# Four equal first chunks, constants on another queue, and two steps moved back in a decoder layer on one core

## Chip, cores, metric

The kernel runs on one core of a Trainium2 chip. The metric is the device time of one execution in microseconds (us). A core has TensorE (matrix products; the profile calls it PE, and PEld its weight loads), VectorE (DVE), ScalarE (ACT), GpSimd (POOL) and SyncE (SP). Here SyncE only issues transfers. ScalarE can issue transfers too, on a queue of its own. Products accumulate in eight banks of 512 float32 columns each.

## What is computed

One layer of a decoder, for 512 tokens of width 1024, all in float32:

```python
x = x + token_mixer(rmsnorm(x, norm_mix_g), w_in, fox_b_f, t5_bias, w_gate, w_branch, w_out)
x = x + conv_ffn(rmsnorm(x, norm_ffn_g), w_up, conv_w, conv_b, w_down)
return rmsnorm(x, norm_final_g)

def rmsnorm(x, g):
    return x * rsqrt(mean(x * x, axis=-1) + 1e-6) * g

def token_mixer(xn, ...):
    proj = xn @ w_in          # queries, keys, values of four mixers, forget gate, indexer
    # stick-breaking, MoBA, forgetting (FoX) and indexer-selected (DSA) attention
    mixed = sum(sigmoid(xn @ w_gate[i]) * (branch[i] @ w_branch[i]) for i in range(4))
    return mixed @ w_out
```

FoX adds to each score the difference of a running sum c of log-sigmoids of its gate logits: + c at the query, - c at the key.

## The kernel before, in words

Each float32 operand is split into a high part (a rounded copy in the format that TensorE takes) and a low part (the rest), and each product is done as three: high by high, low by high, high by low.

**The start.** x arrives transposed, as eight blocks of 128 features by 512 tokens. The first product wants the values of FoX and DSA and the indexer's weights: 328 columns of w_in, also in eight blocks. `CHUNKS` (L880) cuts both into chunks; each chunk of x goes to `xr`, each chunk of weights to `w0r` (L191 to L195). The 28 columns of constants that are wanted first (the norms' gains among them) and the four constant matrices go to `cst` (L190, L196). SP issues nearly all of this, ScalarE two weight chunks. Meanwhile TensorE does nine products of zeros (L199, `WARM`). For every block, ScalarE multiplies x by the gain of the feature, which gives the high part `xhi` (L224), and VectorE makes the low part `xlo` (L227); ScalarE casts the chunk's weights to `w0h` (L226), VectorE makes `w0l` (L229). TensorE then does, chunk by chunk, the three products of each block with four tiles of 128 tokens (L233).

**The mean of squares.** The products take x before its division by the root mean square, and `rstd` is multiplied in later. ScalarE squares x in pairs of blocks (L238), VectorE adds the squares (L242, L244), and a product with a constant matrix (L279) gives the mean over features. `rms_rstd` (L137 to L148) makes rstd of it on ScalarE and VectorE. This product stands behind the first six of the 24 products of the projection `dk` (L276 to L279; DSA key, indexer key and forget gate). The generator of a projection pauses after every six products.

**The projections.** Projections (`proj`, L258) write in turn to two banks (tag "mm"): dk, ix0, ix1, F0q, F0k and so on, so that ix1 takes the bank of dk and F0k that of ix1. After dk, VectorE multiplies rstd in (L266), takes rstd to token rows (L285), and dk's bank is read by copies for `kD` and `ixk` (L363 to L367) and last by the forget gate's first step (L390). `ixtile` (L355) does one of two indexer query projections: rstd on VectorE (L266), high part `iqs` on ScalarE (L358), low part on VectorE (L359), and a transfer to a scratch in DRAM (L360).

**The decay rows.** From the gate row come c's high and low parts `ch` (L399, L400) and their negation `cn` (L401), and both go to DRAM (L402, L403). `fox_fill` (L311) later copies rows of them into the FoX queries and keys.

TensorE's order is that of the program text. The instructions of the other engines are put in order by a scheduler that simulates a timeline, within what data, buffers, `tc.high_priority` and `tc.issue_after` (not before that instruction is issued) allow. Big weights stream through two raw buffers from L100, are cast by ScalarE (L90) and completed by VectorE or GpSimd (L91). After the mixers come the gates, the branch products, the output projection and the feed-forward part.

Of the kernel before, what the change touches and what calls it, by code (L numbers as in the profile page):

```python
# [12 lines left out]
AF = mybir.ActivationFunctionType  # L13
# [3 lines left out]
P = 128  # L17
# [27 lines left out]
def fr(ap):  # L45
    return ap.bitcast(F32)
# [3 lines left out]
def trunk(ctx: ExitStack, tc: tile.TileContext, xt, wv0, wv, wp, wdk, wg, wb, wo, wu, wd,  # L50
          convp, foxb, t5, onehot, consts, ymask, out):
    nc = tc.nc
    V, A, G, T, SP = nc.vector, nc.scalar, nc.gpsimd, nc.tensor, nc.sync
# [7 lines left out]
    cst = cp.tile([P, NCST], F32, name="cst")  # L61
# [44 lines left out]
    def weight(hold=1, ahead=2):  # L106

        i = used[0]
        used[0] += hold
        while len(ready) < min(len(stream), i + hold + ahead):  # L110
            emit_weight()
        return ready[i] if hold == 1 else ready[i:i + hold]

    def dense_steps(o, hi, lo, xh, xl, kt=KT, late=False, chunk=6):


        blocks = [range(kt - 1), [kt - 1]] if late else [range(kt)]
        todo = [(a, b, k) for ks in blocks for a, b in ((hi, xh), (hi, xl), (lo, xh)) for k in ks]
        for n, (a, b, k) in enumerate(todo):
            T.matmul(o, a[:, k], b(k), start=(n == 0), stop=(n == len(todo) - 1))  # L120
            if n % chunk == chunk - 1:
                yield chunk * S / 2400.0

    def blocks_of(t):
        return lambda k: t[:, k]
# [4 lines left out]
    def bank(name, tag="a"):  # L130
        return psum.tile([P, S], F32, name=name, tag=tag, bufs=6 if tag == "a" else 2)
# [46 lines left out]
    with ExitStack() as ph:  # L178
# [8 lines left out]
        w0d = wv0.rearrange("p (k n) -> p k n", k=KT)  # L187
        w0r = []
        with tc.high_priority(offset=5000):
            SP.dma_start(cst[:, 4 * P:], consts[:, 4 * P:NCST])  # L190
            for a, b in CHUNKS:  # L191
                SP.dma_start(xr[:, :, a:b].rearrange("p h k t -> p h (k t)"),
                             xt[:, :, a:b, :].rearrange("h p k t -> p h (k t)"))
                w0r.append(hp.tile([P, b - a, NV0], F32, name=f"w0r{a}", tag="w0r", bufs=4))
                (SP if a > 1 else A).dma_start(w0r[-1], w0d[:, a:b])  # L195
            SP.dma_start(cst[:, :4 * P], consts[:, :4 * P])  # L196
        A.preload_act_table_set("natural_log_exp_and_others")
        wps = bank("wps")
# [22 lines left out]
        sqs, last_hi = [], []  # L221
        for c, (a, b) in enumerate(CHUNKS):
            for k in range(a, b):
# [6 lines left out]
            for m, (x, w) in enumerate(((xhi, w0h), (xlo, w0h), (xhi, w0l))):  # L230
                for k in range(a, b):
                    for tt in range(NB):
                        T.matmul(vps[tt], x[:, k, tt * P:(tt + 1) * P], w[:, k], start=(m == 0 and k == 0),  # L233
                                 stop=(m == 2 and k == KT - 1))
        for c, (a, b) in list(enumerate(CHUNKS))[1:]:
            sq = hp.tile([P, 2, S], F32, name=f"sq{b}", tag="sq", bufs=4)
            with tc.issue_after(last_hi[min(c + 1, len(CHUNKS) - 1)]):
                A.activation(sq.rearrange("p k (h t) -> p h k t", h=2), xr[:, :, b - 2:b], AF.Square)  # L238
            sqs.append(sq)
            if len(sqs) > 1:  # L240
                with tc.issue_after(last_lo):
                    V.tensor_tensor(out=sqs[0], in0=sqs[0], in1=sq, op=OP.add)  # L242
# [15 lines left out]
        def proj(name, m=P):  # L258

            hi, lo = weight()  # L260
            ps = bank(f"d{name}", "mm")
            yield from dense_steps(ps[:m], hi, lo, blocks_of(xhi), blocks_of(xlo))
            return ps[:m]

        def factored(ps):
            V.tensor_tensor(out=ps, in0=ps, in1=rstd[:ps.shape[0]], op=OP.mult)  # L266
            return ps

        def drain(gen):
            while True:  # L270
                try:
                    next(gen)
                except StopIteration as e:
                    return e.value

        dk = proj("dk", 100)  # L276
        next(dk)
        ms = bank("ms")
        T.matmul(ms, onesd, sqa, start=True, stop=True)  # L279
# [75 lines left out]
        def ixtile(c):  # L355
            t = factored(drain(proj(f"ix{c}")))
            hl = pp.tile([P, 2, S], F32R, name=f"iqs{c}", tag="lo", bufs=HB)
            A.copy(hl[:, 0], t)  # L358
            V.tensor_tensor(out=hl[:, 1], in0=t, in1=fr(hl[:, 0]), op=OP.subtract)  # L359
            SP.dma_start(iqd[4 * c:4 * c + 4].rearrange("h b x s -> (h b) x s"), fr(hl))  # L360

        kD = pp.tile([P, 1, 2, S], F32R, name="kD")
        A.copy(kD[0:64, 0, 0], dkp[0:64])  # L363
# [6 lines left out]
        SP.dma_start(fr(kD[64:128, 0]), fr(kD[0:64, 0]))  # L370

        ixtile(0)

        for c0, c1 in ((0, 512), (512, 640)):
# [14 lines left out]
        R4 = slice(96, 100)  # L389
# [7 lines left out]
        ch = pp.tile([P, 2, S], F32R, name="ch", tag="hi", bufs=HB)  # L397
        cn = pp.tile([P, 2, S], F32R, name="cn", tag="lo", bufs=HB)
        A.copy(ch[R4, 0], fw[R4, 0])  # L399
        V.tensor_tensor(out=ch[R4, 1], in0=fw[R4, 0], in1=fr(ch[R4, 0]), op=OP.subtract)  # L400
        A.activation(cn[R4], fr(ch[R4]), AF.Copy, scale=-1.0)  # L401
        SP.dma_start(crd[0], fr(ch[R4]))  # L402
        SP.dma_start(crd[1], fr(cn[R4]))  # L403

        ixtile(1)

        def bias_head(h):
            e = pp.tile([P, S], F32, name=f"e{h}", tag="e", bufs=3)
# [230 lines left out]
        for pr in ("F0", "S0", "F1", "S1", "M0", "M1", "D0", "D1"):  # L639
            nm, b = pr[0], "FMSD".index(pr[0])  # L640
# [207 lines left out]
    for f in range(KT):  # L848
        ch = weight(3, 1)
# [27 lines left out]
PRIO = 60  # L877
RBUFS, WBUFS = 2, 3
HB = 3
CHUNKS = ((0, 1), (1, 2), (2, 4), (4, 6), (6, 8))  # L880
WARM = 9
NV0 = 328
DCH = ((0, 8), (8, 8), (16, 6))
# [13 lines left out]
NCST = 4 * P + 3 * KT + 4  # L897
# [95 lines left out]
```

## Time and profile before

| | us |
|---|---|
| median of three runs | 857.58 (857.57 to 859.62) |
| the profiled execution | 857.41 |
| its span, first to last instruction | 855.6 |
| TensorE busy | 837.3 |
| VectorE busy | 538.1 |
| ScalarE busy | 398.8 |
| GpSimd busy | 164.6 |

The profile is one execution. Its times count from the start of the span. In a timeline's row stand the start, the time that the row's instructions took, the engine, the line of the kernel, the operation, output and inputs by name, shapes and count; in brackets how long the engine had idled before it and what ended that. A group of like instructions stands in one row. Engine "SPq" is SP's issuing of transfers. In a row of windows stand each engine's busy time in that stretch with the number of instructions, then the clock that TensorE was granted (1.00 is 2.4 GHz, 0.50 is 1.2 GHz), the share of the transfer engines' time and the GB/s moved.

### The profile page before, as it was taken

How to read it: one execution, taken by the hardware profiler on the slowest of the kernel's cores; microseconds unless marked ns; L12 is line 12 of the kernel's file. 1: busy time of each engine (PE TensorE's matmuls, PEld its weight loads, DVE VectorE, ACT ScalarE, POOL GpSimd, SP SyncE). 2: the span in 40 equal slices, each digit the busy share in tenths (PEclk: the TensorE clock that was granted, in tenths of full speed). 3: DMA queues.
4: the chain of work that ended last, by engine and by line, in shares of the span. 5: the costliest groups of instructions: out<-in, count | busy, mean ns of one | idle time of the engine just before them, and what ended most of it. 6: DMA issues, size and time to landing. Idle time of an engine off the chain costs nothing.

```text
span 855.6 us, 10625 instructions
## 1 busy us (share of the span) xinstructions
PE 837.3 (98%) x4019; PEld 702.2 (82%) x4019; DVE 538.1 (63%) x931; ACT 398.8 (47%) x612; POOL 164.6 (19%) x131
## 2 busy tenths in 40 slices
PE   8999999999999999999999999999999999999995
PEld 7778887888888888888888888888888888888885
DVE  5947899996453468455554477777777777333234
ACT  6556785664554843232344454444444444232231
POOL 1244575377568300000001200000000000000000
PEclk9999999999999999999999999999999999999998
DMA  6567334326332243232223223333333333333322
GB/s 227 167 163 178 100 132 108 87 58 189 90 120 74 75 130 117 74 103 96 77 74 107 89 98 98 99 99 99 98 99 99 98 97 91 90 93 93 90 65 98
DMA packets 31667, 90.68 MB, mean 106 GB/s; under 512 B 3384, under 2 KB 8376, under 8 KB 31616
## 3 DMA queue, kind: packets, MB, share of 16 engines
q1 hardware_dynamic: 30240, 88.62, 34.3%
q10 hardware_dynamic: 1376, 1.38, 0.5%
q8 instruction: 31, 0.51, 0.2%
q14 instruction: 20, 0.16, 0.1%
HBM read 83.78 MB, written 5.82 MB: 105 GB/s over the span
## 4 chain that ended last, share of the span: by engine, by line
PE 80%; DVE 1%; POOL 0%; ACT 0%; issue 0%; DVEq 0%; POOLq 0%
PE u L120 28%; PE dg L120 19%; PE dn L833 14%; PE o L120 5%; PE b L120 5%; PE vpsVM L303 1%; PE dM1q L120 1%; PE dM1k L120 1%; PE zb L545 1%; PE dD1q L120 1%; PE dD0q L120 1%; PE ptD L484 1%; PE ptM L484 1%; PE dM0q L120 0%; PE oD L500 0%; PE oM L500 0%
## 5 line engine op out<-in xcount | busy, mean ns | idle before, releaser
L90 ACT CAST wh<-wr 128x1024 fp32r<-128x1024 f32 (+1 forms) x129 | 133.7, 1039 | 153.8 <-PE dn L833 70.4
L91 DVE TENSOR_TENSOR wl<-wr,wh 128x1024 fp32r<-128x1024 f32 (+2 forms) x97 | 116.3, 1200 | 138.6 <-ACT wh L90 63.6
L120 PE MATMUL u<-xhi,wh 128*128 128x512 f32 x352 | 87.5, 390 | 0.0
L91 POOL TENSOR_TENSOR wl<-wr,wh 128x1024 fp32r<-128x1024 f32 x32 | 77.0, 2408 | 52.9 <-PE dix L120 15.3
L120 PE MATMUL u<-xlo,wh 128*128 128x512 f32 x352 | 87.1, 389 | 0.0
L120 PE MATMUL u<-xhi,wl 128*128 128x512 f32 x352 | 87.1, 389 | 0.0
L809 DVE SCALAR_TENSOR_TENSOR cv<-h,cvp,cv 128x511 f32<-128x511 f32 x88 | 66.0, 751 | 26.2 <-ACT cv L807 24.6
L120 PEld LDWEIGHTS u<-xhi,wh 128*128 128x128 f32 x352 | 66.1, 188 | 14.1 <-issue 0.5
L120 PEld LDWEIGHTS u<-xlo,wh 128*128 128x128 f32 x352 | 66.1, 188 | 13.7
L120 PEld LDWEIGHTS u<-xhi,wl 128*128 128x128 f32 x352 | 66.1, 188 | 13.7
L807 ACT ACTIVATE cv<-h,cvp 128x512 f32<-128x512 f32 x44 | 35.9, 815 | 79.8 <-DVE h L805 79.8
L833 PE MATMUL dn<-mh,wh 128*128 128x512 f32 (+1 forms) x198 | 72.9, 368 | 0.0
L833 PE MATMUL dn<-ml,wh 128*128 128x512 f32 (+1 forms) x198 | 72.3, 365 | 0.0
L833 PE MATMUL dn<-mh,wl 128*128 128x512 f32 (+1 forms) x198 | 72.3, 365 | 0.0
L120 PE MATMUL dg<-xlo,wh 128*128 128x512 f32 x256 | 66.1, 392 | 0.0
L120 PE MATMUL dg<-xhi,wh 128*128 128x512 f32 x256 | 64.9, 390 | 0.0
L120 PE MATMUL dg<-xhi,wl 128*128 128x512 f32 x256 | 64.3, 390 | 0.0
L120 PEld LDWEIGHTS dg<-xhi,wl 128*128 128x128 f32 x256 | 47.7, 188 | 9.8
L120 PEld LDWEIGHTS dg<-xhi,wh 128*128 128x128 f32 x256 | 47.8, 188 | 9.4
L120 PEld LDWEIGHTS dg<-xlo,wh 128*128 128x128 f32 x256 | 47.4, 188 | 9.5
L781 POOL TENSOR_TENSOR rstd<-rstd,sqo 128x512 f32<-128x512 f32 x7 | 9.1, 1302 | 187.1 <-ACT sqo L780 187.1
L833 PEld LDWEIGHTS dn<-ml,wh 128*128 128x128 f32 x198 | 37.3, 188 | 6.2
(430 smaller groups left out, 1453.0 us busy)
## 6 DMA issues: line engine op xcount, KB each, us to landing
wr<-in_wu SPq DMA_DIRECT2D x44, 512.0 KB
wr<-in_wg SPq DMA_DIRECT2D x32, 512.0 KB
wr<-in_wp SPq DMA_DIRECT2D x16, 512.0 KB
wr<-in_wd SPq DMA_DIRECT2D x16, 512.0 KB
wbr<-in_wb SPq DMA_DIRECT2D x8, 512.0 KB
wr<-in_wo SPq DMA_DIRECT2D x8, 512.0 KB
wr<-in_wd SPq DMA_DIRECT2D x8, 384.0 KB
bdram<-brd SPq DMA_DIRECT2D x2, 1280.0 KB
```

Source lines behind the costliest of these rows:

```text
L90: A.copy(hi, raw)
L91: eng.tensor_tensor(out=lo, in0=raw, in1=fr(hi), op=OP.subtract)
L120: T.matmul(o, a[:, k], b(k), start=(n == 0), stop=(n == len(todo) - 1))
L303: T.matmul(ps, a[:, k, ts_], b, start=(m == 0), stop=(m == 3 * KT - 1))
L484: T.transpose(pt[:, (i - j) * P:(i - j + 1) * P], z[:, QOFF[i] + P * j:QOFF[i] + P * (j + 1)], ident)
L545: T.matmul(zs[j][:, P * (j2 - j):n], trir if j2 == j else negr, x[:, KOFF[j2]:KOFF[j2] + n2], start=False, stop=(j2 == NB - 1 and x is ll) ...
L781: G.tensor_tensor(out=acc, in0=acc, in1=sq, op=OP.add)
L807: A.activation(c, h, AF.Identity, scale=cvp[:, i, 2:3], bias=cvp[:, i, 3:4])
L809: V.scalar_tensor_tensor(out=c[:, x:], in0=h[:, :S - x], scalar=cvp[:, i, 2 - x:3 - x], in1=c[:, x:], op0=OP.mult, op1=OP.add)
L833: T.matmul(o, a, b[:, k, cs], start=(n == 0 and m == 0), stop=(n == ND - 1 and m == 2))
```

## The change

x and the first weights come in four chunks of two blocks instead of two of one block and three of two. SP's first transfer is x. ScalarE issues the first weight chunk and then the 28 columns of constants; SP issues the other weight chunks. The squares still come in four pairs of blocks. A second `next(dk)` puts twelve of dk's products ahead of the mean of squares. `ixtile` returns the instruction that makes the high part, and the negation `cn` is issued only after that of ix1; ix1's projection now stands ahead of the negation and its transfer in the text.

```diff
@@ -187,12 +187,13 @@
         with tc.high_priority(offset=5000):
-            SP.dma_start(cst[:, 4 * P:], consts[:, 4 * P:NCST])
             for a, b in CHUNKS:
                 SP.dma_start(xr[:, :, a:b].rearrange("p h k t -> p h (k t)"),
                              xt[:, :, a:b, :].rearrange("h p k t -> p h (k t)"))
                 w0r.append(hp.tile([P, b - a, NV0], F32, name=f"w0r{a}", tag="w0r", bufs=4))
-                (SP if a > 1 else A).dma_start(w0r[-1], w0d[:, a:b])
+                (SP if a else A).dma_start(w0r[-1], w0d[:, a:b])
+                if a == 0:
+                    A.dma_start(cst[:, 4 * P:], consts[:, 4 * P:NCST])
             SP.dma_start(cst[:, :4 * P], consts[:, :4 * P])
@@ -232,7 +233,7 @@
-        for c, (a, b) in list(enumerate(CHUNKS))[1:]:
+        for c, (a, b) in enumerate(CHUNKS):
@@ -274,6 +275,7 @@
         dk = proj("dk", 100)
+        next(dk)
         next(dk)
         ms = bank("ms")
@@ -355,9 +357,10 @@
-            A.copy(hl[:, 0], t)
+            hi = A.copy(hl[:, 0], t)
             V.tensor_tensor(out=hl[:, 1], in0=t, in1=fr(hl[:, 0]), op=OP.subtract)
             SP.dma_start(iqd[4 * c:4 * c + 4].rearrange("h b x s -> (h b) x s"), fr(hl))
+            return hi.ins
@@ -398,11 +401,11 @@
-        A.activation(cn[R4], fr(ch[R4]), AF.Copy, scale=-1.0)
         SP.dma_start(crd[0], fr(ch[R4]))
+
+        with tc.issue_after(ixtile(1)):
+            A.activation(cn[R4], fr(ch[R4]), AF.Copy, scale=-1.0)
         SP.dma_start(crd[1], fr(cn[R4]))
-
-        ixtile(1)
@@ -877,7 +880,7 @@
-CHUNKS = ((0, 1), (1, 2), (2, 4), (4, 6), (6, 8))
+CHUNKS = ((0, 2), (2, 4), (4, 6), (6, 8))
```

## Rows read from the trace of the kernel before

**Rows 1.** The page's table of busy time: TensorE.

```profile
PE 837.3 (98%) x4019; PEld 702.2 (82%) x4019; DVE 538.1 (63%) x931; ACT 398.8 (47%) x612; POOL 164.6 (19%) x131
```

**Rows 2.** Who waited for whom, TensorE, whole span: total, times, longest.

```profile
PE vpsVM L303 <- DVE vvM L211: 1.3, 1, 1.3
```

**Rows 3.** Timeline of all engines, 0 to 40 us: TensorE's first products.

```profile
1.32 4.16 PE L200 MATMUL wps<-warm 128*128 128x512 f32 x9 [1.32 <-POOL warm L186]
...
6.75 0.87 PE L233 MATMUL vps<-w0h,xhi 128*128 128x328 f32 x4 [1.28 <-ACT xhi L224]
...
11.42 1.47 PE L233 MATMUL vps<-w0h,xhi 128*128 128x328 f32 x8 [0.65 <-ACT w0h L226]
```

**Rows 4.** TensorE's timeline, 21 to 30 and 34 to 49 us.

```profile
22.34 1.54 PE L120 MATMUL ddk<-xhi,wh 128*100 128x512 f32 x6
24.59 1.12 PE L279 MATMUL ms<-sqa,cst 128*128 128x512 f32 x2 [0.71 <-DVE sqa L244]
...
36.43 2.11 PE L120 MATMUL dix<-xhi,wh 128*128 128x512 f32 x8
...
48.08 1.21 PE L120 MATMUL dF0k<-xhi,wh 128*128 128x512 f32 x4 [0.48 <-DVE iqs L359]
```

**Rows 5.** Timeline of all engines, 0 to 40 us: SP's issues and ScalarE.

```profile
0.74 0.40 SPq L190 DMA_DIRECT2D cst<-in_consts  x1
...
1.20 1.45 SPq L192 DMA_DIRECT2D xr<-in_xt  x3
...
5.98 0.72 ACT L224 ACTIVATE xhi<-xr,cst 128x512 fp32r<-128x512 f32 x1 [2.28 <-DMA xr<-in_xt]
...
7.51 0.73 ACT L224 ACTIVATE xhi<-xr,cst 128x512 fp32r<-128x512 f32 x1 [0.46 <-DMA xr<-in_xt]
...
12.23 1.32 ACT L224 ACTIVATE xhi<-xr,cst 128x512 fp32r<-128x512 f32 x2
...
15.05 1.32 ACT L224 ACTIVATE xhi<-xr,cst 128x512 fp32r<-128x512 f32 x2
```

**Rows 6.** Windows at the start: last column GB/s.

```profile
0.00:2.00 2.00, 0.68 (x2) 0.59 (x3) 0.25 (x3) 0.33 (x1) 1.36 (x7) 1.00 0.07 9
0.00:5.60 5.60, 4.16 (x9) 2.81 (x9) 0.75 (x4) 1.75 (x2) 2.81 (x9) 1.00 0.63 157
0.00:7.50 7.50, 4.90 (x13) 3.40 (x13) 1.52 (x6) 2.83 (x4) 2.81 (x9) 1.00 0.70 181
8.00:11.00 3.00, 2.78 (x19) 2.51 (x17) 1.59 (x3) 1.84 (x4) 0.00 (x0) 1.00 1.05 408
```

**Rows 7.** Timelines of VectorE and ScalarE, 26 to 49 us.

```profile
27.54 0.69 DVE L144 SCALAR_TENSOR_TENSOR tm<-ms,rstd 128x512 f32<-128x512 f32 x1
...
35.28 0.76 DVE L390 TENSOR_SCALAR fw<-ddk,fb 4x512 f32<-4x512 f32 x1
...
43.62 1.98 DVE L400 TENSOR_TENSOR ch<-fw,ch 4x512 fp32r<-4x512 f32 x1
47.33 0.69 DVE L359 TENSOR_TENSOR iqs<-dix,iqs 128x512 fp32r<-128x512 f32 x1 [1.73 <-ACT iqs L358]
...
45.63 1.06 ACT L401 ACTIVATE cn<-ch 4x1024 fp32r<-4x1024 f32 x1 [2.13 <-DVE ch L400]
46.72 0.59 ACT L358 CAST iqs<-dix 128x512 fp32r<-128x512 f32 x1
```

**Rows 8.** Window from the first FoX keys to 200 us.

```profile
48.00:200.00 152.00, 147.61 (x833) 127.35 (x834) 127.05 (x319) 102.96 (x190) 83.77 (x55) 1.00 0.44 121
```

**Rows 9.** Windows at the end of the span: granted clock before the last two columns.

```profile
842.00:845.00 3.00, 3.00 (x28) 3.00 (x27) 2.77 (x5) 0.00 (x0) 0.00 (x0) 1.00 0.35 115
845.00:848.00 3.00, 1.08 (x6) 0.47 (x4) 0.78 (x2) 1.30 (x3) 0.00 (x0) 1.00 0.70 235
848.00:849.00 1.00, 0.00 (x0) 0.00 (x0) 0.90 (x3) 0.00 (x1) 0.00 (x0) 0.68 0.00 0
849.00:855.00 6.00, 0.00 (x0) 0.00 (x0) 2.87 (x5) 0.00 (x0) 0.00 (x0) 0.50 0.53 175
```

## The prediction

> **What bounds the kernel now.** I read the page's table of busy time first. TensorE works for nearly the whole span [rows 1], so the change can win only what TensorE now idles or spends out of turn. The list of TensorE's waits is second: twelve causes, none over 1.3 us [rows 2], some 9 us in all. Four lie before 48 us, where the change acts, and TensorE's own timeline dates them. The first product of the real weights starts at 6.75 after 1.28 us of idling, the third chunk (blocks 2 and 3) at 11.42 after 0.65 [rows 3], the mean of squares at 24.59 after 0.71, and the projection of the first FoX keys at 48.08 after 0.48 [rows 4]. Then come ScalarE's timeline, which shows when each chunk of x was in hand [rows 5], the bytes moved by then [rows 6], and VectorE's and ScalarE's timelines between 27 and 48 us, which show what the later starts depend on [rows 7].
>
> The profiled execution took 857.41 us, span 855.6 and 1.8 around it, 0.17 under the median of the three runs, 857.58. I make the sum in microseconds won or lost in the profile and apply it to the median. What a measurement of this kernel can tell from no change is about 0.3%, 2.57 us.
>
> **Step 1, the first transfers.** The constants leave the head of SP's queue, so x is issued at 0.74 instead of 1.20 [rows 5]; on ScalarE's queue they take the place of the second weight chunk, so ScalarE issues two transfers as before. Chunk 0 is now 512 KB of x and 328 KB of weights; with 14 KB of constants that is 874 kB. The first product needs all of x's chunk where it needed half.
>
> When is that in hand? By 5.60 us the queues had moved 5.60 x 157 = 879 kB [rows 6]: were every byte for chunk 0, it would be there at about 5.6, the early bound. The late bound is the old kernel itself: the second block of x, the last of the same bytes, released ScalarE at 7.51 [rows 5]. I take the middle, 6.55: the first end has no straggler, in the second later chunks have mixed in, and the new case is neither. The Trainium skill (DMA: Bandwidth & Descriptors, section Anatomy of one DMA) gives a transfer a fixed part of about 2 us and the rest at 436 GB/s: an estimate from that page has 874 kB there 4 us after the issue, near 5.1, and the sum would be 855.4, close to the second rival below. The rows gave 157 to 181 GB/s on average up to there [rows 6].
>
> The constants follow 328 KB of weights on ScalarE's queue, and every scaling of x reads a gain from them. I cost this at nothing, because x's 512 KB should end later than the 342 KB there. If that cover fails, the loss is bounded by the same 7.51: by then the old kernel had all these bytes.
>
> **Step 2, the chunk stage.** TensorE followed ScalarE's first scaling by 0.77 us (5.98 to 6.75) [rows 3, 5], so its first product starts at 7.32 (6.37 to 8.28). From the third chunk on, nine groups of eight products took 11.42 to 22.34, 1.213 us each [rows 3, 4]. Twelve such groups are 14.56 and end at 21.9 (20.9 to 22.85), against 22.34. Removed are the 0.65 us wait and small gaps, added is the later start. Call the shift s: **-0.45 us**, between -1.4 and +0.5. ScalarE went round a middle chunk in 2.82 us (12.23 to 15.05) [rows 5] against TensorE's 3.64, so it keeps up.
>
> **Step 3, the mean of squares.** It now stands behind twelve products of the first projection instead of six. A product of 512 columns takes 0.233 us (48 of them from 36.43 to 47.60) [rows 4]. The mean of squares started 2.25 us after that projection (22.34 to 24.59); six products are 1.40, so 0.85 was lost there, and the later place removes it. But twelve products take 2.80, so it starts 0.55 us later, plus s. All of rstd's chain on VectorE hangs on it, from 27.54 to the end of the forget-gate row at 35.28 + 0.76 = 36.04 [rows 7], and VectorE's instructions follow close on one another in between. That row is the last reader of the bank into which the second indexer projection (ix1) writes: the small banks alternate between two, and dk and ix1 share one. TensorE would reach ix1 at 36.43 - 0.85 + s = 35.13, while the bank comes free at 36.04 + 0.55 + s = 36.14. It waits a microsecond there, and with 0.06 for the release (47.33 + 0.69 to 48.08 [rows 4, 7]) starts at 36.20. So steps 2 and 3 together are worth 36.43 - 36.20 = **0.23 us**; the 0.85 has turned into a wait ten microseconds later. At the ends of s the pair gives a gain of 1.18 or a loss of 0.72.
>
> **Step 4, the negated rows.** Now ScalarE does the negation (45.63, 1.06 us) ahead of ix1's high part (46.72), though its input is ready only when VectorE ends the decay's low part at 43.62 + 1.98 = 45.60 [rows 7]. ix1's high part waits behind it, its low part follows at 47.33, and the bank that this frees lets the first FoX keys go at 48.08, 0.48 late [rows 4, 7]. With the high part first, ScalarE does it in the idle 2.1 us before 45.63, and the low part can end near 46.3. TensorE arrives near 47.4, so the whole **0.48 us** goes. Behind the negation stand its transfer, on SP the copies of the decay rows and the next weights, on ScalarE a weight cast. It still starts when its input ends, so I cost these at nothing; were it to follow the high part late, by its 0.59 us [rows 7], the cover is that the rows are not read before the first scores, after the whole projection of the FoX keys.
>
> **Step 5, after 48 us.** VectorE is busy 127.05 of 152 us up to 200 [rows 8], and TensorE waits on chains that start from its own results. I let the gain pass whole.
>
> Sum: -0.23 - 0.48 = -0.71, or **856.9 us**. Its own range runs from 857.58 - 1.18 - 0.48 = 855.9 to 857.58 + 0.72 - 0.48 = 857.8.
>
> **The rivals.**
>
> *The array's clock falls before the first product: slower.* The idling between the warm-up (done at 1.32 + 4.16 = 5.48) and the first product grows from 1.28 to 1.84 us, at most 2.8 [rows 3]. At the end of this trace TensorE was full to 845, worked 1.08 us of the next three, and the granted clock then fell from 1.00 to 0.50, the 1.2 GHz level, within the microsecond from 848 [rows 9]. So a gap of 1.28 us did not do it, three microseconds with little work did, and the new gap lies between. The warm-up ran at 4.16 / 9 = 0.46 us a product, twice 0.233, for 4.16 us. If the first real products ran at that level as long, half of it, 2.08 us, would be lost: 856.9 + 2.08 = **859.0**. The Trainium skill (TensorE: Matmul & The Clock Gate, section HAM oscillation — how this bites in real kernels) says that an array kept waiting by transfers between bursts is throttled again and starts the next burst cold; by that rule this rival would be the forecast. The old gap did not show it, the end of the trace did. Chance 0.20; it decides if the first product comes at the late end of step 2.
>
> *The first transfers run at the later rate.* If the short rows of the two small chunks made the start slow, 874 kB at the 408 GB/s of 8 to 11 us take 2.1 us; next to nothing has moved by 2.0 [rows 6], so they are there near 4.1. Then s is -2.9, and the sum 857.58 - 2.9 + 0.22 - 0.48 = **854.4**. Against it, 7.50 x 181 = 1357 kB had moved by 7.50 [rows 6], some 480 of them from the third chunk with its long rows, and the average was still so low. Chance 0.07.
>
> *VectorE has more room than I think.* All engines but TensorE are put in order by the program's scheduler, and an order with the forget-gate row earlier would spare the wait of step 3. Then -0.45 - 0.85 - 0.48 = -1.78, **855.8**; with the early bound of step 1, 854.85. VectorE's packed row speaks against it [rows 7]. Chance 0.08.
>
> *Nothing arrives at the end.* The gain is eaten between 48 and 200 us, where VectorE is nearly full [rows 8] and a wait such as the 1.3 us for the MoBA values [rows 2] grows by as much, or a late landing costs in steps 2 and 3 what step 4 wins: **857.6**. Chance 0.15.
>
> **How the numbers follow.** The forecast has 0.50. Faster than 855.0 needs the rate rival (0.05 of its 0.07), VectorE's room with an early landing (0.02) or an order of the other engines that I can't see (0.03): 0.10. Slower than 860.15 needs the low clock for longer together with a late landing (0.04), or a worse order (0.03): 0.07. Within 0.3%: 0.83. The range leaves out the faster cases below and the low clock with a late landing above, about 0.10 on either side: 855.0 to 859.3.
>
> **What would show it.** Right: ScalarE's first scaling near 6.6 and released by x, TensorE's twelve groups in 14.6 us without a stop, no wait at the mean of squares, a new wait of about 1 us ahead of ix1, none ahead of the FoX keys, and those near 47.4. Wrong: a first scaling at 7.5 or released by the constants, early groups of 2.4 us, no wait ahead of ix1, another order on VectorE before 40 us, or TensorE's waits after 48 us grown by what was won.

## The result and the profile after

The changed kernel takes 862.61 us (median of 6 runs, 860.55 to 865.13), the one before 857.58 (6 runs, 857.38 to 859.62). The ratio is 1.0057 [1.0034, 1.008], slower, and the median lies above the range given. Ratios and intervals here are those of the comparison itself, not quotients of medians. The profiled execution took 861.86 us, span 860.1, against 855.6 before: 4.5 us to be found in one trace.

The page's table of busy time, the row that answers to [rows 1]:

```profile
PE 840.1 (98%) x4019; PEld 705.5 (82%) x4019; DVE 537.2 (62%) x930; ACT 398.5 (46%) x611; POOL 164.3 (19%) x131
```

TensorE does the same 4019 products, but is busy 2.8 us longer: part of the loss is products that ran more slowly. The rest is waiting, and the list of who waited for whom (total, times, longest) has a new first row; the 1.3 us of [rows 2] stand unchanged below it:

```profile
PE dix L120 <- DVE fw L393: 3.5, 1, 3.5
```

The timeline of the changed kernel dates it. First ScalarE and TensorE at the start (answering to [rows 3, 5]), then TensorE from dk to the first FoX keys (answering to [rows 4]):

```profile
1.21 0.45 ACTq L196 DMA_DIRECT2D cst<-in_consts  x1
1.32 4.21 PE L201 MATMUL wps<-warm 128*128 128x512 f32 x9 [1.32 <-POOL warm L186]
5.92 1.34 ACT L225 ACTIVATE xhi<-xr,cst 128x512 fp32r<-128x512 f32 x2 [0.41 <-DMA cst<-in_consts]
6.70 2.56 PE L234 MATMUL vps<-w0h,xhi 128*128 128x328 f32 x8 [1.17 <-ACT xhi L225]
9.05 1.79 PE L234 MATMUL vps<-w0h,xlo 128*128 128x328 f32 x8
...
22.68 2.00 PE L120 MATMUL ddk<-xhi,wh 128*100 128x512 f32 x8
25.45 1.02 PE L281 MATMUL ms<-sqa,cst 128*128 128x512 f32 x2
34.62 1.24 PE L379 MATMUL bp<-vt,t5s 32*8 32x512 f32 x4
39.37 3.75 PE L120 MATMUL dix<-xhi,wh 128*128 128x512 f32 x8 [3.51 <-DVE fw L393]
47.13 1.98 PE L120 MATMUL dF0q<-xhi,wh 128*128 128x512 f32 x8
52.57 0.61 PE L120 MATMUL dF0k<-xhi,wh 128*128 128x512 f32 x2
```

The kernel before began its FoX queries, which follow ix1, here:

```profile
42.00 1.98 PE L120 MATMUL dF0q<-xhi,wh 128*128 128x512 f32 x8
```

Read as a ledger against [rows 4], in us lost:

| stretch | before | after | lost |
|---|---|---|---|
| up to dk | 22.34 | 22.68 | +0.34 |
| dk until TensorE is free for ix1 | 14.09 (to 36.43) | 13.18 (to 39.37 - 3.51 = 35.86) | -0.91 |
| wait ahead of ix1 | 0 | 3.51 | +3.51 |
| ix1's 24 products | 42.00 - 36.43 = 5.57 | 47.13 - 39.37 = 7.76 | +2.19 |
| FoX queries, then the keys | 48.08 - 42.00 = 6.08 | 52.57 - 47.13 = 5.44 | -0.64 |
| sum, at the first FoX keys | 48.08 | 52.57 | +4.49 |

The moves themselves did what they were for: no wait stands at the mean of squares or at the FoX keys. The loss is one place, ix1. Why does its bank come free so late? VectorE's timeline of the changed kernel:

```profile
34.79 1.22 DVE L91 TENSOR_TENSOR wl<-wr,wh 128x1024 fp32r<-128x1024 f32 x1 [0.42 <-ACT vvF L211]
35.93 0.69 DVE L267 TENSOR_TENSOR dix<-dix,rstd 128x512 f32<-128x512 f32 x1
36.53 0.48 DVE L212 SCALAR_TENSOR_TENSOR vvF<-vps,rst,vvF 128x256 fp32r<-128x256 f32 x1
37.04 0.69 DVE L370 TENSOR_TENSOR ixk<-ddk,ixk 32x512 fp32r<-32x512 f32 x1
37.76 0.68 DVE L380 TENSOR_TENSOR vt<-vt,bp 8x512 f32<-8x512 f32 x1
38.47 0.76 DVE L393 TENSOR_SCALAR fw<-ddk,fb 4x512 f32<-4x512 f32 x1
```

and of the kernel before, right behind its forget-gate row at 35.28 [rows 7]:

```profile
36.07 1.22 DVE L91 TENSOR_TENSOR wl<-wr,wh 128x1024 fp32r<-128x1024 f32 x1
37.32 0.70 DVE L266 TENSOR_TENSOR dix<-dix,rstd 128x512 f32<-128x512 f32 x1
...
38.97 0.86 DVE L377 TENSOR_TENSOR vt<-vt,bp 8x512 f32<-8x512 f32 x2
```

Three instructions that stood behind the bank's last reader, fw, now stand ahead of it: the weights' low part 1.22, ix0's rstd 0.69 and the bias row 0.68, together 2.59 us. The first of them comes after 0.42 us of idling, for a vvF of ScalarE. (Of VectorE's own four vvF, three stand ahead of fw in either kernel.) No line of the diff touches these three. The program's scheduler, which orders all engines but TensorE, chose anew once TensorE's order had changed.

The windows of the changed kernel say why ix1 then ran slowly (busy time of PE, PEld, DVE, ACT, POOL, then PEclk, the granted clock, DMA share and GB/s). The last one answers to [rows 8]:

```profile
35.00:37.00 2.00, 0.86 (x4) 0.17 (x2) 2.00 (x3) 1.40 (x5) 0.00 (x0) 1.00 0.53 113
37.00:38.00 1.00, 0.00 (x0) 0.00 (x0) 0.94 (x3) 0.46 (x2) 0.00 (x0) 0.64 0.69 131
38.00:39.30 1.30, 0.00 (x0) 0.00 (x0) 1.24 (x3) 0.04 (x1) 0.00 (x0) 0.50 0.84 328
39.30:44.00 4.70, 4.63 (x11) 3.69 (x12) 4.43 (x13) 2.41 (x5) 0.00 (x0) 0.50 0.33 123
44.00:45.00 1.00, 1.00 (x5) 0.81 (x5) 0.52 (x1) 0.45 (x1) 0.00 (x0) 0.94 0.00 0
...
48.00:200.00 152.00, 147.63 (x833) 127.31 (x832) 123.67 (x306) 101.94 (x184) 84.10 (x54) 1.00 0.42 117
```

Within the pause the granted clock fell from 1.00 to 0.50, the 1.2 GHz level, and it stayed there while ix1 worked without a gap, until just after 44. After 48 us the product count and the busy time of the old kernel are back.

### The profile page after: what moved, and what is told of

The parts are those of the page before. It is cut to its first block, busy times and chain, and to the rows that moved or that the text cites. A ratio compares the mean times of both kernels' runs of the same rounds, so it can differ in the third digit from the quotient of the medians.

```text
span 860.1 us, 10620 instructions
## 1 busy us (share of the span) xinstructions
PE 840.1 (98%) x4019; PEld 705.5 (82%) x4019; DVE 537.2 (62%) x930; ACT 398.5 (46%) x611; POOL 164.3 (19%) x131
## 4 chain that ended last, share of the span: by engine, by line
PE 80%; DVE 1%; POOL 0%; ACT 0%; issue 0%; DVEq 0%; POOLq 0%
PE u L120 28%; PE dg L120 19%; PE dn L836 14%; PE o L120 5%; PE b L120 5%; PE vpsVM L305 1%; PE dM1q L120 1%; PE dM1k L120 1%; PE zb L548 1%; PE dD1q L120 1%; PE dD0q L120 1%; PE ptD L487 1%; PE ptM L487 1%; PE dM0q L120 0%; PE oD L503 0%; PE oM L503 0%
## 5 line engine op out<-in xcount | busy, mean ns | idle before, releaser
L836 PEld LDWEIGHTS dn<-mh,wh 128*128 128x128 f32 x198 | 37.3, 188 | 6.2
```

What stands on the lines that cost most here:

```text
L836: T.matmul(o, a, b[:, k, cs], start=(n == 0 and m == 0), stop=(n == ND - 1 and m == 2))
```

## The experiments

The theory from this trace: the second `next(dk)` alone costs over 4 us, by VectorE's new order and the clock that falls in the pause. The rivals: the chunks cost something too, by late constants or by a low clock at the start; the negation costs or wins something else than its 0.48. The kernel before had medians of 857.63, 857.45 and 857.60 in the three groups of runs (experiments 1 to 4; 5 to 8; 9 to 12), and 857.58 beside the change. Where medians of different groups are compared below, up to 0.2 us of the difference can be the group's.

**1. The mean of squares alone** (against the kernel before):

```diff
         next(dk)
+        next(dk)
```

> Only the second step of dk ahead of the mean of squares, all else as before. Theory (the later mean of squares makes the scheduler put the forget gate's first step behind other work on VectorE, the bank of ix1 comes free some 3.5 us late, and TensorE's clock falls in that pause): 861 to 864.5 us, a wait of 3 to 4 us ahead of ix1, released by the forget gate's step, and a stretch of 1.2 GHz that starts in or just behind it. Rival (the larger first chunks cost the time): 856.5 to 858.5 us and a wait of at most 1.2 us there.

Measured: 861.95 (860.31 to 862.22, 5 runs), ratio 1.0037 [1.0023, 1.005]. Its timeline has the same wait of the same length:

```profile
39.48 3.75 PE L120 MATMUL dix<-xhi,wh 128*128 128x512 f32 x8 [3.51 <-DVE fw L391]
```

One line makes the wait, without the chunks and without the negation. From the start of dk to the FoX keys this trace takes 30.02 us (22.79 to 52.81) where the kernel before took 25.74, 4.28 more; by the medians the line costs 4.32, by the ratio 3.2. VectorE's new order, with the three instructions ahead of fw, was found in the change and in experiments 1, 6 and 9. The kernels without the second `next(dk)` lack it, and so do experiments 5 and 11, which have that line but free the bank.

The start of this trace shows one thing more. Its chunks are the old ones and its first product came after a pause of 1.02 us, and yet the first four products took 1.26 us (6.55 to 7.81), where the kernel before took 0.79: a low clock at the start does not need the larger chunks.

**2. The negation alone** (against the kernel before):

```diff
-        A.activation(cn[R4], fr(ch[R4]), AF.Copy, scale=-1.0)
...
-        ixtile(1)
+        with tc.issue_after(ixtile(1)):
+            A.activation(cn[R4], fr(ch[R4]), AF.Copy, scale=-1.0)
```

> Only the negation behind ix1's high part. Theory: 857.58 - 0.48 = 857.1 us, the wait of 0.48 us ahead of the first FoX keys gone and nothing else moved. Rival (the gain is eaten between 48 and 200 us): 857.6 us with the wait gone and other waits of TensorE grown by as much.

Measured: 857.07 (856.52 to 858.78, 11 runs), ratio 0.9995 [0.9986, 1.0004]. The time alone can't be told from no change; its timeline can:

```profile
47.46 1.98 PE L120 MATMUL dF0k<-xhi,wh 128*128 128x512 f32 x8
...
86.36 3.50 PE L120 MATMUL dF1q<-xhi,wh 128*128 128x512 f32 x8
```

The wait of 0.48 [rows 4] is gone, and ix1 had started at 36.45, as before. But this execution was the slowest of the eleven, 858.78, with a span of 857.0: it lost again more than it had won. TensorE waited 0.4 us for the indexer queries to come back from DRAM (iq from iqd), a wait that the list of the kernel before does not have, and at about 86.5 the granted clock fell:

```profile
87.00:90.00 3.00, 3.00 (x8) 2.31 (x8) 2.48 (x6) 0.90 (x3) 2.79 (x6) 0.52 0.82 266
```

The eight products from 86.36 took 3.29 us to the next group, in the kernel before 1.86. Three of the eleven runs lie near 858.7, the others at 857.22 or less; whether the other two slow ones had the same fall was not traced.

**3. The chunks alone** (against the kernel before; constants and chunks as in the change):

```diff
-            SP.dma_start(cst[:, 4 * P:], consts[:, 4 * P:NCST])
...
+                if a == 0:
+                    A.dma_start(cst[:, 4 * P:], consts[:, 4 * P:NCST])
...
-CHUNKS = ((0, 1), (1, 2), (2, 4), (4, 6), (6, 8))
+CHUNKS = ((0, 2), (2, 4), (4, 6), (6, 8))
```

> Only the four equal chunks, with the constants on ScalarE's queue. Theory (the mean of squares costs the time): 856.5 to 858.5 us, VectorE's order as before, no wait over 1 us ahead of ix1. Rival (the chunks cost it, by a first product that finds TensorE at 1.2 GHz): 859.5 to 862 us, with the loss in the products before 23 us.

Measured: 860.04 (858.8 to 861.45, 11 runs), ratio 1.0023 [1.0014, 1.0033]. My expectation fell, the rival's held. Timeline of ScalarE, then of TensorE:

```profile
5.88 0.74 ACT L227 CAST w0h<-w0r 128x656 fp32r<-128x656 f32 x1 [2.84 <-DMA w0r<-in_wv]
7.75 2.56 ACT L225 ACTIVATE xhi<-xr,cst 128x512 fp32r<-128x512 f32 x4 [1.13 <-DMA cst<-in_consts]
...
8.52 2.56 PE L234 MATMUL vps<-w0h,xhi 128*128 128x328 f32 x8 [2.99 <-ACT xhi L225]
...
25.48 1.55 PE L120 MATMUL ddk<-xhi,wh 128*100 128x512 f32 x6
```

The 14 KB of constants, issued at 1.23, released ScalarE only at 7.75, 1.87 us behind the weights ahead of them on the same queue. TensorE paused 2.99 us and then ran the first group of eight in 2.35 us (8.52 to 10.87), where a full clock takes 1.21 [rows 3, 4]. So dk began 3.1 us late. The change's own trace had hardly shown this: in that execution the constants released ScalarE at 5.92.

What moved meanwhile, from 5.42 to 7.30 (queue; packets, MB, share of the transfer engines' time; q1 is SP's, q10 ScalarE's):

```profile
q1 hardware_dynamic: 232, 0.47, 84.8%
q10 hardware_dynamic: 128, 0.01, 5.8%
```

The weights were through by then, and the packets of the constants went out a few at a time beside SP's transfers. The landings recorded in the same trace, told apart by the order of issue and by when their readers were released, have the first chunk of x complete at 6.18 and the constants at 7.66: x was not what was missing.

**4. Chunks and negation, the change without the second `next(dk)`:**

```diff
-        next(dk)
```

> The change without the second step of dk ahead of the mean of squares: four equal chunks and the negation behind ix1's high part. Theory: 856 to 858 us, 4 to 6 us under the whole change; the sum of what chunks alone and negation alone give. Rival (the chunks cost the time): 859 to 861.5 us.

Measured: 859.07 (858.1 to 859.74, 11 runs), ratio 1.0013 [1.0004, 1.0022]; again the rival's figure.

```profile
7.88 1.34 ACT L225 ACTIVATE xhi<-xr,cst 128x512 fp32r<-128x512 f32 x2 [1.51 <-DMA cst<-in_consts]
...
48.83 1.98 PE L120 MATMUL dF0k<-xhi,wh 128*128 128x512 f32 x8
```

Late constants again, and no wait at the FoX keys. By medians the parts alone cost 4.32 (mean), 2.41 (chunks) and -0.56 (negation), 6.17 in all; the change costs 5.03. So they add up to within 1.1 us, while the change's own runs spread over 4.6.

**5. The whole change, dk's bank freed early.** dk times rstd goes to a tile of SBUF instead of back into the bank, so the bank's last reader is that product and not the forget-gate row (against the change):

```diff
-        dkp = factored(dkp)
+        dks = pp.tile([P, S], F32, name="dks", tag="ir", bufs=3)
+        V.tensor_tensor(out=dks[:100], in0=dkp, in1=rstd[:100], op=OP.mult)
+        dkp = dks
```

> The whole change, but VectorE writes dk times rstd to SBUF, so that dk's bank is free after one instruction and the forget gate's step is no longer what ix1 waits for. Theory (the bank's last reader is the wait of 3.5 us and through it the fall of the clock): the wait ahead of ix1 gone, no stretch of 1.2 GHz between 30 and 50 us, 856.5 to 859.5 us. Rival (the later rstd holds up whatever comes next, bank or not): a wait of 2 us or more at another projection before 60 us and 860.5 us or more.

Measured: 859.12 (856.25 to 860.05, 12 runs), ratio 1.001 [1.0, 1.0021], 3.5 us under the change. Timeline and windows of this kernel:

```profile
8.04 1.33 ACT L225 ACTIVATE xhi<-xr,cst 128x512 fp32r<-128x512 f32 x2 [1.93 <-DMA cst<-in_consts]
...
8.82 2.55 PE L234 MATMUL vps<-w0h,xhi 128*128 128x328 f32 x8 [3.60 <-ACT xhi L225]
...
39.20 2.11 PE L120 MATMUL dix<-xhi,wh 128*128 128x512 f32 x8
```

```profile
8.00:15.00 7.00, 6.18 (x23) 6.18 (x24) 5.66 (x8) 6.96 (x11) 0.00 (x0) 0.51 1.05 405
...
38.00:44.00 6.00, 6.00 (x26) 4.25 (x26) 5.94 (x15) 5.36 (x12) 0.00 (x0) 1.00 0.57 154
```

With the bank free, ix1 follows the bias products without a wait and at the full clock: the wait and the low clock at 37 to 44 have one cause. The edit changes VectorE's order too (fw now comes at 35.55, ahead of ix0's rstd, the weights' low part and the bias row), so it does not part the bank from the order. That the bank is the link is read from the release in the change's trace, `<-DVE fw`, and from the program, in which dk's bank is all that fw and ix1 share. What is left is the start: the nine warm-up products took 3.90 us instead of 4.21, so the last of them had run at the higher clock; then TensorE stood still for 3.60 us, and from 8 to 15 it ran at half. Its times spread over 3.8 us.

**6. The pause filled with products** (20 of 384 columns into the second bias product's bank, behind that product; nothing reads them):

```diff
+        for i in range(20):
+            T.matmul(bp[:, 128:512], xhi[:, i % KT, :P], xhi[:, i % KT, 128:512], start=True, stop=True)
```

> The whole change, with 20 products of 384 columns (some 3.3 us at full clock) into unused columns of a bank ahead of ix1; their results are read by nothing. Theory (3.5 us of the loss is the wait, 2.2 us the clock that falls in it): ix1 starts as late as with the change, 39.4 or so, but at full clock, and the time is 1.8 to 2.8 us under the change's, 859.5 to 861 us. Rival (the clock's fall has another cause, or costs nothing that is not lost anyway): 862 to 864 us.

Measured: 866.48 (863.81 to 867.73, 5 runs), ratio 1.0096 [1.0081, 1.0112], outside both ranges:

```profile
38.55 5.33 PE L382 MATMUL bp<-xhi 128*128 128x384 f32 x20 [3.73 <-DVE vt L380]
```

VectorE reads that bank too (the bias row at line 380), so the filler waited as long as ix1 had and only came behind the pause. The 20 products themselves took 5.16 us to the next group (38.55 to 43.71), in experiment 9, without a pause ahead of them, 3.68 (34.48 to 38.16): behind this pause too some 1.5 us went to the clock, only not in ix1.

**7. Equal chunks, constants back at the head of SP's queue** (against the kernel before, whose first transfer stays where it was):

```diff
-                (SP if a > 1 else A).dma_start(w0r[-1], w0d[:, a:b])
+                (SP if a else A).dma_start(w0r[-1], w0d[:, a:b])
...
+CHUNKS = ((0, 2), (2, 4), (4, 6), (6, 8))
```

> Only the four equal chunks, with the constants at the head of SP's queue as before. Theory (behind the first weights on ScalarE's queue the constants land last, and every scaling of x waits for them): first scaling released by x at 6 to 6.6 us instead of by the constants at 7.8, and 857.5 to 859.3 us, 1 us or more under chunks alone (860.0). Rival (x's larger first chunk is the late one): first scaling at 7.5 us or later, released by x, and 859.5 us or more.

Measured: 857.04 (856.31 to 857.3, 11 runs), ratio 0.9994 [0.9986, 1.0003]: 3.0 us under the chunks alone (2.8 if each is taken against the kernel before of its own group), and a little better than I had expected.

```profile
5.89 1.33 ACT L224 ACTIVATE xhi<-xr,cst 128x512 fp32r<-128x512 f32 x2 [1.07 <-DMA xr<-in_xt]
...
6.66 2.55 PE L233 MATMUL vps<-w0h,xhi 128*128 128x328 f32 x8 [1.14 <-ACT xhi L224]
```

Now x itself releases the first scaling, and the runs spread over 1.0 us instead of 2.7. The queue of the constants, not the size of the chunks, was the cost.

**8. The chunks alone with a longer warm-up** (against experiment 3):

```diff
-WARM = 9
+WARM = 16
```

> Chunks alone with 16 products of zeros ahead instead of 9, so that TensorE works until some 7 us. Theory (of what chunks cost, over 1 us is the clock at 1.2 GHz behind the longer pause): the first products run at full clock, groups of 1.2 us, and 857.6 to 858.9 us, with the first product still near 8.5. Rival (only the later start counts): 859.5 to 861 us. A third way: zeros do not hold the clock, and nothing changes.

Measured: 857.42 (856.09 to 858.0, 11 runs), ratio 0.9995 [0.9986, 1.0003], 2.6 us under the chunks alone.

```profile
1.32 6.69 PE L201 MATMUL wps<-warm 128*128 128x512 f32 x16 [1.32 <-POOL warm L186]
7.84 1.37 PE L234 MATMUL vps<-w0h,xhi 128*128 128x328 f32 x8
9.06 1.36 PE L234 MATMUL vps<-w0h,xlo 128*128 128x328 f32 x8
```

The first product starts later than in the change's trace (7.84 against 6.70), and still dk begins earlier, at 22.24 against 22.68, because the groups take 1.21 us from the first one on. From the first product to dk it is 14.40 us, in experiment 3 16.96. In this execution, 1.0 us under the kernel's median, the constants landed early (they released ScalarE at 6.22), so it shows the clock and not a late landing that was covered. Experiments 7 and 8 each take back about all that the chunks cost, so the late constants and the low clock are not two costs to be added: the late landing makes the pause, and the pause costs most where the clock is low behind it.

**9. The pause filled ahead of the second bias product** (the same 20 unread products):

```diff
+            for i in range(20 if c0 else 0):
+                T.matmul(bp[:, 128:512], xhi[:, i % KT, :P], xhi[:, i % KT, 128:512], start=True, stop=True)
```

> The whole change, with the same 20 unread products put ahead of the second bias product, so that they don't wait for VectorE's reading of their bank. Theory (2.2 us of the loss is the clock that falls in the wait ahead of ix1): ix1 starts near 39.4 as with the change, no stretch at 1.2 GHz after 30 us, and 859.3 to 861.5 us. Rival (the clock's fall there costs nothing that is not lost anyway): 862 to 864 us.

Measured: 860.38 (858.69 to 861.82, 5 runs), ratio 1.0033 [1.002, 1.0046], 2.2 us under the change.

```profile
34.48 3.74 PE L380 MATMUL bp<-xhi 128*128 128x384 f32 x20
...
38.47 2.12 PE L120 MATMUL dix<-xhi,wh 128*128 128x512 f32 x8
...
44.06 1.98 PE L120 MATMUL dF0q<-xhi,wh 128*128 128x512 f32 x8
```

The useless products end about when the bank comes free (fw ends at 38.14), so ix1 starts no earlier after dk than in the change (16.88 us against 16.69), but its 24 products now take 5.59 us (38.47 to 44.06) instead of 7.76. This prices the fall of the clock apart from the wait: 2.17 us in the trace. The 2.2 between the medians agree, but there the intervals overlap and the starts differ as well (dk began at 21.59 here, at 22.68 in the change's trace).

**10. What the runs recommended so far**: equal chunks, constants on SP, the negation moved, 13 warm-up products, the mean of squares where it was (against the change):

```diff
+            SP.dma_start(cst[:, 4 * P:], consts[:, 4 * P:NCST])
...
-                if a == 0:
-                    A.dma_start(cst[:, 4 * P:], consts[:, 4 * P:NCST])
...
-        next(dk)
...
-WARM = 9
+WARM = 13
```

> The parts that should pay: four equal chunks with the constants at the head of SP's queue, the negation behind ix1's high part, 13 products of zeros instead of 9, the mean of squares where it was. Theory: 857.04 (chunks with the constants on SP) less 0.48 for the wait ahead of the first FoX keys, less 0.5 to 1.5 for the first groups at full clock: 855 to 856.1 us. Rival (gains of this size are eaten before the end): 856.7 to 857.5 us.

Measured: 856.1 (855.36 to 857.22, 11 runs), ratio 0.9985 [0.9976, 0.9994], at the upper end of what I had expected.

```profile
23.54 1.13 PE L279 MATMUL ms<-sqa,cst 128*128 128x512 f32 x2 [0.71 <-DVE sqa L244]
...
46.39 1.98 PE L120 MATMUL dF0k<-xhi,wh 128*128 128x512 f32 x8
```

**11. The same with the mean of squares moved and dk's bank freed** (experiment 10 with the second `next(dk)` and the three lines of experiment 5):

```diff
+        next(dk)
...
-        dkp = factored(dkp)
+        dks = pp.tile([P, S], F32, name="dks", tag="ir", bufs=3)
+        V.tensor_tensor(out=dks[:100], in0=dkp, in1=rstd[:100], op=OP.mult)
+        dkp = dks
```

> The same with the mean of squares behind twelve products and dk's bank freed after one instruction. Theory (with equal chunks TensorE no longer waits for the squares, so the later place has nothing to win, and with the bank free nothing to lose): within 0.5 us of the kernel without it. Rival (the later place still wins its 0.85 us): 0.6 us or more faster than that kernel.

Measured: **854.93** (854.54 to 855.26, 7 runs), ratio 0.997 [0.9959, 0.9981], the best kernel here, and 1.17 us under experiment 10. No run of it is as slow as the fastest of experiment 10. I had expected the two to be within half a microsecond; the rival was right.

```profile
24.26 1.02 PE L280 MATMUL ms<-sqa,cst 128*128 128x512 f32 x2
34.60 2.11 PE L120 MATMUL dix<-xhi,wh 128*128 128x512 f32 x8
45.62 1.98 PE L120 MATMUL dF0k<-xhi,wh 128*128 128x512 f32 x8
```

The wait of 0.71 is gone and nothing takes its place: the FoX keys start 0.77 us earlier than in experiment 10, and 0.97 counted from dk, which began 0.20 later. My expectation had gone by traces with equal chunks in which dk began at 22.24 or later and no wait stood at the mean of squares (experiments 3, 4, 7 and 8); in experiment 10 dk begins at 21.29, and the wait is back. All three ideas of the change win something in the traces, once each one's side effect is taken away; by the times alone only this one is clear, while the chunks (experiment 7) and the negation (experiment 2) stay within the noise.

**12. The kernel before with 13 warm-up products** (`WARM = 13`):

> The kernel before with 13 products of zeros instead of 9. Theory (the old kernel's pause of 1.3 us ahead of the first product is mostly short enough): 856.7 to 857.5 us, with fewer executions near 859. Rival (the clock cost the old kernel as much as the new): 855 to 856.3 us.

Measured: 857.35 (856.73 to 859.01, 11 runs), ratio 1.0001 [0.9993, 1.001]. The old start had little to win from a longer warm-up, and two of the eleven executions still lie near 859, so a longer warm-up does not remove those. With the equal chunks the warm-up does count: dk begins at 21.29 in experiment 10, at 22.90 in experiment 7, whose first group ran at half speed. How the gain of experiments 10 and 11 divides between the warm-up and the rest was not measured.

## Why the prediction was wrong, step by step

**Step 1, the failing sentence is "I cost this at nothing"**, for the constants behind the first weights. The cover named was x's chunk, thought to land later than the weights and constants together. In all seven traces with the change's own order of transfers (the change and experiments 3 to 6, 8 and 9) it was the constants that ended ScalarE's wait, at 5.92 to 8.04 us, though by the recorded landings x's chunk was complete at 5.52 to 6.18, earlier than the 6.55 that I took; the 7.75, 7.88 and 8.04 of experiments 3 to 5 lie beyond even the bound of 7.51 that I gave for the case without cover. I reckoned in bytes ahead in the queue, and 14 KB weigh nothing that way. Experiment 7 undoes this alone: 3.0 us. The Trainium skill's rule that I quoted (DMA: Bandwidth & Descriptors, section Anatomy of one DMA — SWDGE (gpsimd) path: about 2 us and the bytes at 436 GB/s) is given there for transfers that GpSimd issues, which I did not say; here SP and ScalarE issue them. An estimate by it would have the constants there near 3.2, 2.03 us after their issue; the change's trace has the issue at 1.21 and the release at 5.92, so the trace does not agree.

**Step 2, the shift s.** -0.45 forecast, +0.34 in the profiled execution, inside the bounds of -1.4 to +0.5 but for another reason. The first product came at 6.70, earlier than the 7.32 forecast. But the first group took 2.35 us and the second 1.63 (9.05 to 10.68), so the twelve groups took 22.68 - 6.70 = 15.98 us instead of 14.56. That is the clock rival, to which I gave 0.20, though on its condition it was wrong: the pause was 1.17 us, shorter than the old 1.28. In this execution the clock had not yet risen when the first product began (the column of the granted clock prints 1.00 in a window from 7 to 10, as it does in [rows 6] under the warm-up products, which take 0.46 us each; the real products take twice the time of [rows 3], and I go by them); the fall in a longer pause that I had described is what experiment 5 shows. Where the clock had risen, the sum was right: in experiment 9 the twelve groups take 14.52 us (7.07 to 21.59) and s is -0.75. But in the traces with this start s reaches +3.75 (experiment 5), far beyond the bound of +0.5, which rested on the cover of step 1.

**Step 3, right mechanism, mis-sized term, which is the largest part of the miss.** I predicted a new wait ahead of ix1, on the bank of dk, ended by the forget-gate row, and it is there. I made it about 1 us; it is 3.51, and 2.19 more go to the clock that falls in it. The failing assumption was that VectorE would run the same list of instructions, shifted by 0.55 + s. By that, fw would start at 35.28 + 0.55 + 0.34 = 36.17; it started at 38.47, 2.30 later, because of the three instructions now ahead of it. I had a rival on the scheduler's order, but only as a gain ("VectorE has more room", 0.08), and gave "a worse order" 0.03. Experiment 1 shows that the one line does it (+4.3 us), experiment 5 that the wait goes when the bank is freed (-3.5), experiment 9 that the clock's part is 2.2. The 0.85 that I reckoned for the later place is real: 0.77 at the FoX keys in experiment 11, 0.97 from dk on, where the bank no longer stands against it.

Of the 5.20 us between the forecast start of the FoX keys (48.08 - 0.71 = 47.37) and the measured 52.57, 2.44 are the longer wait (3.51 for 36.20 - 35.13 = 1.07), 2.19 the clock behind it and 0.79 the shift s; the rest, -0.26, are small terms that came out better.

**Step 4, right.** The wait of 0.48 at the first FoX keys is gone in experiments 2 and 4 and in the change: 857.07 in experiment 2 against the 857.1 that its expectation gave. As forecast, the gain by itself is too small for the measurement to tell. The keys gain 0.64 (the ledger's last stretch), 0.16 more than the row's wait, since a group's time as printed runs past the start of the next: from start to start a product takes 0.227 us (24 in 5.44), not the 0.233 that I had from ends. I had costed what stands behind the negation at nothing. The wait of 0.4 us for iq from iqd is in the traces of experiments 2 and 6, and in none of the other six kernels with the later negation, nor in any without it; whether the negation brings it is open.

**Step 5, right in kind.** What is gained or lost by 48 us passes whole: +4.49 at the first FoX keys, +4.5 in the span, and within 0.2 us in eleven of the twelve experiments. The exception is the traced execution of experiment 2: 0.62 gained at the keys, 1.4 lost in the span, most of it where the clock fell, behind 86 us.

**The range** failed since two cases that I held unlikely, a worse order (0.03) and a low clock (0.20, at the start), come from one cause and arrive together: the pause that the order makes is the pause in which the clock falls. I had put the clock's risk at the start alone, and had not asked whether the new wait that I myself predicted was long enough for it. At the 1 us that I took it would not have been, by the 1.28 of [rows 3]; the question of how long it could become was never asked.

**Left open.** Why the constants' landing differs so much between executions of one order (released at 5.92 to 8.04) is not settled, nor why the scheduler puts fw later with the second `next(dk)`, and not where dk's bank is freed. Constants on ScalarE's queue ahead of its weights were not tried. The spread of the changed kernel's own six runs (4.6 us) is put down to the landing and the clock at the start; that it shrinks to 0.7 in experiment 11 agrees, but single executions of the change were not traced apart.

## What to carry to other kernels

Put a transfer that everything waits for at the head of a queue, however small it is: here that took back 2.8 to 3.0 us, and the bytes ahead of it were a poor measure of when it landed. Where a scheduler orders an engine, a step moved by hand on another engine can reorder the work around a shared bank; name the bank's last reader, and free the bank early (a copy out instead of a product in place) before moving anything toward it. A wait on TensorE as long as those seen here (3.1 to 3.7 us in the change and in experiments 1, 4, 5 and 6) is to be priced twice, once as the wait and once for the half clock behind it.

## What the runs showed of the hardware that was not expected

- **A pause is paid for after it ends.** TensorE's last work ahead of the pause ended at 34.62 + 1.24 = 35.86; the granted clock was 0.64 in the window from 37 to 38, 0.50 from 38 to 44 and 0.94 in the next microsecond. TensorE had been at work again since 39.37, 4.63 us of it at half the clock, so the price was 2.19 us on top of the 3.51 of waiting. The Trainium skill (TensorE: Matmul & The Clock Gate, section HAM oscillation — how this bites in real kernels) says that an array left waiting between bursts is throttled and begins the next burst cold; the traces agree for the pauses of 3.51 here and 3.60 in experiment 5, while behind the 1.61 at the start of experiment 9 and the 1.28 of [rows 3] the products run at full speed. In experiments 4 and 6 the fall came later, some 0.7 us after the work had begun again behind pauses of 3.13 and 3.73. And a fall does not need so long a pause: in experiment 2 the clock fell at about 86.5, where the longest wait of TensorE in the two microseconds ahead was 0.56 us, the same as in the kernel before, where it did not fall. Why is open.
- **After nine warm-up products the clock had risen in some executions and not in others.** Seven traces have nine of them and a pause of less than 2 us ahead of the first product. Where the nine took 4.21 us (the change, experiments 1 and 7), the first group behind them runs at half speed: 2.35 and 2.36 us for eight products, 1.26 for the four of experiment 1. Where they took less (4.16 in the kernel before, 3.81, 4.09 and 4.14 in experiments 2, 6 and 9), it does not. With 13 to 16 of them, the first groups took 1.2 to 1.33 us in each of experiments 8, 10 and 11.
- **14 KB landed some two microseconds behind 328 KB.** In experiment 3 the constants were issued right behind the weights on one queue, and released their reader 1.87 us after the weights released theirs. At the head of SP's queue they ended no wait (experiments 7, 10 and 11).
